# A decoder trunk on one core: casts of operand sums moved between the first products of the gates, pinned on ScalarE

## Chip, core and metric

The kernel runs on one core of a Trainium2 chip. The metric is the time of one execution in device microseconds. Before the change three runs took 1092.08, 1084.63 and 1091.85 us; their median is 1091.85 us.

## What is computed

One layer of a hybrid decoder, for 1024 prompt tokens and 8 x 4 sample tokens, all in float32:

```
h = rms(x);  z = h @ w_in                  # q, k, v and pooling columns
mix = concat(attention(q, k, v), pooling(u)) @ w_out
x = x + rms(mix)
f = rms(x);  f = (silu(f @ w_gate) * (f @ w_up)) @ w_down
x = x + rms(f)
x = x + sigmoid(x @ w_ple_gate) * (p @ w_ple)
```

The model width is 1024, p is 256 wide. The last line, the gates of the per-layer input, is where most of the change lies; its x is the sum x + rms(f) of the line before.

## The kernel before

**Tiles.** Features lie on the partitions, tokens along the free dimension, in three blocks of 352 tokens (g = 0, 1, 2). A tile called a half holds four of the eight feature groups of one block, 128 x 4 x 352; it lies in one of 28 slots. Every float32 operand of a matmul is split in a high part (a cast on ScalarE) and a low part (source minus high part on VectorE); a product is then three matmuls, high by high, high by low, low by high. `split` (L166) makes such a pair, at L167 (ScalarE) and L168 (VectorE).

**Seven products for four.** For blocks 0 and 1 together, the large matrix products are made in the 2 x 2 scheme with seven products instead of eight. Its operands on the token side are B11 and B21 (the two halves of block 0), B12 and B22 (those of block 1), and differences T1 to T4 of them. On the weight side it needs sums S1 to S4 of quarters of the weight, which GpSimd adds in place (L1123 for the gates, L339 for the down projection). Block 2 is multiplied directly.

**The down projection** is a list of steps, one per product and set of weight slabs, each made by `down7` (L1262). The last step of each product adds its four PSUM banks to kept tiles (`add`, L1276). Before the last steps of P2, S2 and S4, one addition of a whole half puts P1 and the kept partial sum of that product together.

**The normed residual** of each block comes from `ple_steps(g)` (L1339), a generator. It is handed to `chain`, and `turn` runs it piece by piece between matmuls by an estimate of VectorE's load; `finish` runs out what is left of it. For block 1 its end also makes the differences for the gates: `e_sum` (L1321) subtracts two halves on VectorE (L1330), `e_high` (L1332) casts the high part on ScalarE (L1335) and returns the function that makes the low part on VectorE (L1337).

**The gates.** First block 2: `ple_out` (L1440) for eight output groups, each followed by an embedding of block 0 (p @ w_ple, L1420 copies it out of PSUM). Then blocks 0 and 1. `ple_first` (L1454) makes, for the output groups a = 7, 5, 3, 1, a first product with B11, copies it to the kept tile p1 (L1463, ScalarE), yields, and then adds the product with B21 in the same PSUM bank; this second product therefore has to wait for the copy. `ple_end` (L1423) puts the sigmoid (L1433, ScalarE) and the two VectorE operations behind it (L1436: times the embedding; L1437: plus the residual), and SP sends the result out (L1438). The four first products are interleaved with each other and with embeddings of block 1 (`embeds`, L1512) at L1516 to L1529. Last comes `ple_rest` (L1468) for four pairs of output groups, with the other five products; these use T1 to T4, and the weight sums of `w_sums` (L1113), which are split at L167 and L168. The first pair's sums are made early; for the second, third and fourth, GpSimd's additions follow a split of half a raw weight (tile w), because they overwrite that raw weight.

**Order.** Each engine runs its instructions in a fixed order, which a scheduler of the framework chooses from the program's order and its own estimates. `tc.keep_in_program_order` pins an instruction at its place in the program. Matmuls are pinned by a flag. The names below end in numbers: b are PSUM banks, u halves of the down projection's sums (and later T1 to T4, in their places), fh and fl high and low parts, wh and wl those of weights, sh and sl those of weight sums, w halves of a weight's pair, p first products, pp embeddings, sg and yo the gates' results.

Of the kernel before, what the change touches and what calls it, by code (L numbers as in the profile page):

```python
# [61 lines left out]
def trunk_kernel(  # L62
# [316 lines left out]
    chains = []  # L379
# [867 lines left out]
    sums7 = {}  # L1247
# [14 lines left out]
    def down7(n):  # L1262
# [12 lines left out]
        def add(out, a, b):  # L1275
            ve.tensor_tensor(out, a, b, op=ALU.add)  # L1276

        onto = {"P2": "P2", "S2": "P1", "S4": "P1"}.get(k, k) if final else k
        if final and k in ("P2", "S2", "S4"):
            add(sums7[onto], sums7["P1"], sums7[k])  # L1280

        def part(j, e):
            wh, wl = need(WDN[k, e], 2)
            x = xops[OPERAND[k], e]
# [8 lines left out]
        for j in range(4):  # L1293
            if len(at) > 2:
                part(j, at[-1])
            else:
                banks[j] = bank()
                for e in at:
                    part(j, e)
            v = banks[j][:, :N]  # L1300
            u = {q: t[:, j, :] for q, t in sums7.items()}

            if n < len(FIVE + TWO):
                se.copy(u[k], v)  # L1304
            else:
                add(u[onto], u[onto], v)
            if final and k in ("P2", "S4"):
                finished(j, int(k == "S4"))
# [23 lines left out]
    def e_high(name):  # L1332
        src = {"T1": os_[0][0], "T2": os_[1][0], "T3": os_[0][1], "T4": os_[1][1]}[name]
        hi, lo = half(0, F32R, "fh"), half(0, F32R, "fl")
        se.copy(hi, src)  # L1335
        e7[name] = hi, lo
        return lambda: ve.tensor_tensor(lo, src, hi.bitcast(F32), op=ALU.subtract)  # L1337

    def ple_steps(g):  # L1339

        pl = half(g, F32R, "pl")
        pls[g] = pl[:, 0:2, :], pl[:, 2:4, :]
        for k in range(2):
            pr = tmp(NS[g], "pr")
            load(pr, p[:, k, OFF[g] : OFF[g + 1]])
            split(pl[:, k, :], pl[:, 2 + k, :], pr)
        x2s[g] = []
        for h in range(2):
            x2[g][h] = half(g, s="x2")
            load(x2[g][h], x1d[g][h])  # L1350
        r = yield from rstd_steps(acc3[g], 24 if g == 1 else 12)
        for h in range(2):
            yh, xh = os_[g][h], x2[g][h]
            ve.tensor_tensor(yh, yh, bc4(r), op=ALU.mult)
            ve.tensor_tensor(xh, xh, yh, op=ALU.add)
            yield 20, 0
            if g == 2:
                x2s[g].append(f_operand(xh, g))
            elif (g, h) != (1, 0):
                e7[f"B{h + 1}{g + 1}"] = f_operand(xh, g)  # L1360
            yield 10, 0
        if g == 1:
            lows = []
            for total, high, low in (("T1", (), 0), ("T2", (), 0), ("T4", ("T2",), 0), ("T3", ("T4",), 1), (None, ("T3", "T1"), 1)):
                lows += [e_high(name) for name in high]
                if total:
                    e_sum(total)
                yield 10, 0
                if low:
                    lows.pop(0)()  # L1370
                    yield 10, 0
            for f in lows:
                f()

    def downs(n, halves):
        hid[:] = old_hid
# [138 lines left out]

    next(firsts[0])  # L1516
    next(firsts[1])
    list(firsts[0])
    embeds(W1[7][0], range(4, KC))
    next(firsts[2])  # L1520
    list(firsts[1])
    next(firsts[3])
    list(firsts[2])
    until[0] = len(ITEMS)
    for a, _ in PAIRS[2:]:
        for j in RAW2[a]:
            w_load(j)
    embeds(W1[1][0], range(4))
    list(firsts[3])  # L1529
    finish(list(chains))  # L1530
    for a, b in PAIRS:
        ple_rest(a, b)

# [85 lines left out]
```

## Time and profile before

| | |
|---|---|
| profiled execution, device us | 1092.91 |
| its span, first to last instruction | 1090.8 |
| around the span | 2.1 |
| median of three runs | 1091.85 |
| lowest and highest run | 1084.63, 1092.08 |
| mean granted clock of TensorE | 0.995 |
| busy: PE, VectorE (DVE), ScalarE (ACT), GpSimd (POOL) | 1075.4, 825.4, 525.7, 285.2 us |

Times in the profile count from the first instruction of the span. Rows of the instructions in order of time have the start, the duration, the engine, the line, the operation, the output and inputs, and in brackets how long the engine had been idle before and what ended that. A wait has the engine and line that waited, what it waited for, the total, the number of times and the longest. A stretch has, for each engine, its busy time and number of instructions, then the granted clock of TensorE, the share of the DMA engines, and GB/s. Matmuls overlap: one that shows 0.32 us starts 0.16 us behind the one before it.

### The profile page before, as it was taken

The page shows a single profiled execution, that of the slowest core. Times are in us where ns is not written, and L with a number is a line of the kernel's source. Part 1 is how long each engine was busy: PE and PEld are TensorE (multiplying, and loading weights), DVE is VectorE, ACT ScalarE, POOL GpSimd, SP SyncE. Part 2 cuts the span into 40 slices and gives each one's busy share as a digit, 9 for nine tenths or more (in the row PEclk, how much of TensorE's full clock was granted, in tenths as well). Part 3 has the DMA queues.
Part 4 walks back from the last instruction along what each step waited for, and adds up shares of the span by engine and source line. Part 5 has one row for each costly group of instructions (what it writes and reads, how often), then busy time and mean ns, then how long its engine had stood idle before and what let it go on. Part 6 is the DMA issues. An engine that isn't in the chain of part 4 may idle for free.

```text
span 1090.8 us, 17447 instructions
## 1 busy us (share of the span) xinstructions
PE 1075.4 (99%) x6793; PEld 1058.9 (97%) x6793; DVE 825.4 (76%) x1229; ACT 525.7 (48%) x951; POOL 285.2 (26%) x213
## 2 busy tenths in 40 slices
PE   9999999999999999999999999999999999999898
PEld 8999988899999999999999999999999999999898
DVE  6766388887979767758758659668678777998978
ACT  8522367666755434334434434334335732575542
POOL 1054022200000122323224232332309096202060
PEclk9999999999999999999999999999999999999899
DMA  8221310542734212441533614515777955825422
GB/s 295 67 66 53 104 55 21 194 173 78 252 125 144 89 66 70 153 169 58 204 118 104 229 48 152 188 47 201 262 275 267 366 193 187 314 95 190 126 70 73
DMA packets 54162, 162.01 MB, mean 149 GB/s; under 512 B 5796, under 2 KB 20164, under 8 KB 54080
## 3 DMA queue, kind: packets, MB, share of 16 engines
q1 hardware_dynamic: 52752, 159.13, 41.4%
q10 hardware_dynamic: 1328, 1.77, 0.5%
q8 instruction: 53, 0.87, 0.3%
q14 instruction: 29, 0.24, 0.1%
HBM read 123.02 MB, written 37.86 MB: 147 GB/s over the span
## 4 chain that ended last, share of the span: by engine, by line
PE 94%; DVE 2%; ACT 1%; DMA 1%; issue 0%; SPq 0%; ACTq 0%; DVEq 0%
PE b L126 94%; PE b L120 1%; DVE ql L168 1%; DVE u L1276 1%; DMA xo<-xd 1%; DMA xr<-in_x_dram 0%; ACT a L771 0%; DVE u L1330 0%; DVE acc L921 0%; DVE yo L1437 0%; DVE st L168 0%; DVE a L811 0%; DVE mx L763 0%; ACT a L736 0%; ACT qh L167 0%
## 5 line engine op out<-in xcount | busy, mean ns | idle before, releaser
L126 PE MATMUL b<-fh,wh 128*128 128x352 f32 x716 | 232.1, 324 | 5.2 <-ACT p L1463 5.2
L126 PE MATMUL b<-fh,wl 128*128 128x352 f32 x716 | 232.5, 325 | 0.0
L126 PE MATMUL b<-fl,wh 128*128 128x352 f32 x716 | 230.7, 322 | 0.0
L1123 POOL TENSOR_TENSOR wr<-wr 128x512 f32<-128x512 f32 x47 | 68.4, 1456 | 546.3 <-DVE wl L168 516.0
L168 DVE TENSOR_TENSOR wl<-wr,wh 128x1024 fp32r<-128x1024 f32 (+1 forms) x123 | 162.8, 1326 | 53.2 <-ACT wh L167 52.9
L167 ACT CAST wh<-wr 128x1024 fp32r<-128x1024 f32 (+1 forms) x123 | 126.1, 1027 | 129.3 <-PE b L126 102.8
L126 PE MATMUL b<-xo,qh 128*128 128x352 f32 x616 | 148.2, 322 | 1.2 <-DMA xo<-xd 1.2
L126 PEld LDWEIGHTS b<-fh,wh 128*128 128x128 f32 x716 | 134.7, 188 | 5.4 <-ACT p L1463 5.4
L126 PEld LDWEIGHTS b<-fl,wh 128*128 128x128 f32 x716 | 136.4, 190 | 0.0
L126 PEld LDWEIGHTS b<-fh,wl 128*128 128x128 f32 x716 | 134.9, 188 | 0.0
L126 PE MATMUL b<-fh,sl 128*128 128x352 f32 x416 | 134.7, 324 | 0.0
L126 PE MATMUL b<-fh,sh 128*128 128x352 f32 x416 | 134.4, 323 | 0.0
L126 PE MATMUL b<-fl,sh 128*128 128x352 f32 x416 | 133.6, 321 | 0.0
L126 PE MATMUL b<-h,wh 128*128 128x352 f32 x480 | 111.9, 323 | 1.1 <-ACT h L495 0.8
L126 PEld LDWEIGHTS b<-xo,qh 128*128 128x128 f32 x616 | 107.3, 188 | 1.7 <-ACT u L1304 1.4
L126 PE MATMUL b<-xo,ql 128*128 128x352 f32 x308 | 99.7, 324 | 1.4 <-DVE ql L168 1.4
L339 POOL TENSOR_TENSOR wq<-wq,wq 128x512 f32<-128x512 f32 x44 | 76.5, 1774 | 69.0 <-DVE ql L168 58.9
L167 ACT CAST st<-c 128x352 fp32r<-128x352 f32 x55 | 26.8, 487 | 123.0 <-DVE c L1192 96.8
L168 DVE TENSOR_TENSOR sl<-wr,sh 128x1024 fp32r<-128x1024 f32 x47 | 58.2, 1238 | 35.3 <-ACT sh L167 33.5
L126 PE MATMUL b<-hid,wh 128*128 128x352 f32 x352 | 84.8, 322 | 0.0
L126 PEld LDWEIGHTS b<-h,wh 128*128 128x128 f32 x480 | 82.3, 188 | 2.5 <-DVE h L496 1.2
L126 PEld LDWEIGHTS b<-fl,sh 128*128 128x128 f32 x416 | 79.0, 190 | 0.0
(211 smaller groups left out, 2178.5 us busy)
## 6 DMA issues: line engine op xcount, KB each, us to landing
wr<-in_w_gu_dram SPq DMA_DIRECT2D x64, 512.0 KB, 3.4
xd<-st SPq DMA_DIRECT2D x35, 704.0 KB, 5.1
xo<-xd SPq DMA_DIRECT2D x35, 704.0 KB, 5.9
wr<-in_w_dn_dram SPq DMA_DIRECT2D x22, 512.0 KB, 4.1
wq<-in_w_dn_dram SPq DMA_DIRECT2D x20, 512.0 KB, 8.6
wr<-in_w_pg_dram SPq DMA_DIRECT2D x10, 512.0 KB, 3.8
x<-in_x_dram SPq DMA_DIRECT2D x6, 704.0 KB, 9.1
x1d<-x SPq DMA_DIRECT2D x6, 704.0 KB, 3.3
```

The source lines that it names most:

```text
L120: ins = te.transpose(out, src, ident)
L126: ins = te.matmul(*args, **kw)
L167: fix(se.copy(hi, src))
L168: fix(ve.tensor_tensor(lo, src, hi.bitcast(F32), op=ALU.subtract))
L339: ge.tensor_tensor(*(q_load(q, e)[:, i, :] for q in (out, a, b)), op=op)
L1123: ge.tensor_tensor(out, a, b, op=op)
L1276: ve.tensor_tensor(out, a, b, op=ALU.add)
```

## The change

```diff
@@ -1276,9 +1276,6 @@
             ve.tensor_tensor(out, a, b, op=ALU.add)
 
         onto = {"P2": "P2", "S2": "P1", "S4": "P1"}.get(k, k) if final else k
-        if final and k in ("P2", "S2", "S4"):
-            add(sums7[onto], sums7["P1"], sums7[k])
-
         def part(j, e):
             wh, wl = need(WDN[k, e], 2)
             x = xops[OPERAND[k], e]
@@ -1299,6 +1296,8 @@
                     part(j, e)
             v = banks[j][:, :N]
             u = {q: t[:, j, :] for q, t in sums7.items()}
+            if j == 0 and final and k in ("P2", "S2", "S4"):
+                add(sums7[onto], sums7["P1"], sums7[k])
 
             if n < len(FIVE + TWO):
                 se.copy(u[k], v)
@@ -1332,7 +1331,7 @@
     def e_high(name):
         src = {"T1": os_[0][0], "T2": os_[1][0], "T3": os_[0][1], "T4": os_[1][1]}[name]
         hi, lo = half(0, F32R, "fh"), half(0, F32R, "fl")
-        se.copy(hi, src)
+        tc.keep_in_program_order(se.copy(hi, src))
         e7[name] = hi, lo
         return lambda: ve.tensor_tensor(lo, src, hi.bitcast(F32), op=ALU.subtract)
 
@@ -1360,17 +1359,9 @@
                 e7[f"B{h + 1}{g + 1}"] = f_operand(xh, g)
             yield 10, 0
         if g == 1:
-            lows = []
-            for total, high, low in (("T1", (), 0), ("T2", (), 0), ("T4", ("T2",), 0), ("T3", ("T4",), 1), (None, ("T3", "T1"), 1)):
-                lows += [e_high(name) for name in high]
-                if total:
-                    e_sum(total)
+            for name in ("T1", "T2", "T4", "T3"):
+                e_sum(name)
                 yield 10, 0
-                if low:
-                    lows.pop(0)()
-                    yield 10, 0
-            for f in lows:
-                f()
 
     def downs(n, halves):
         hid[:] = old_hid
@@ -1515,19 +1506,27 @@
 
     next(firsts[0])
     next(firsts[1])
+    finish(list(chains))
+    low = e_high("T2")
     list(firsts[0])
     embeds(W1[7][0], range(4, KC))
     next(firsts[2])
+    low()
+    low = e_high("T4")
     list(firsts[1])
     next(firsts[3])
+    low()
+    low = e_high("T3")
     list(firsts[2])
     until[0] = len(ITEMS)
     for a, _ in PAIRS[2:]:
         for j in RAW2[a]:
             w_load(j)
+    low()
+    low = e_high("T1")
     embeds(W1[1][0], range(4))
     list(firsts[3])
-    finish(list(chains))
+    low()
     for a, b in PAIRS:
         ple_rest(a, b)
```

The differences T1, T2, T4, T3 are still made by the chain. Their high and low parts are no longer made there: each cast is written behind one of the first products and pinned at its place on ScalarE, and each low part is written one product further on. The chain is finished two first products on, ahead of the first cast, where it was finished behind the last of `ple_first`. In `down7` the whole-half addition is written behind the first PSUM bank of the step instead of ahead of the step. Nothing is added or taken away; the number of instructions on each engine is the same. PE's order is the same too. In the new kernel, lines behind the edits are smaller by up to 9 (L1463 is L1454, L1436 is L1427, L1337 is L1336).

On ScalarE, the place is the end of block 2's gates and the start of the first products. fh_10314 is the last high part of block 1's halves, b_10477 and b_10497 hold the first two first products (b_10464 and b_10483 in the new kernel). Before:

```order
L167 CAST fh_10314<-x_10091 128x1408
L1335 CAST fh_10381<-u_8421 128x1408
L1433 ACTIVATE sg_10405<-b_10359 128x352
L1420 COPY pp_10292<-b_10468 128x352
L1335 CAST fh_10401<-u_8652 128x1408
L1335 CAST fh_10449<-u_8482 128x1408
L1335 CAST fh_10452<-u_8567 128x1408
L1433 ACTIVATE sg_10462<-b_10419 128x352
L1463 COPY p_10476<-b_10477 128x352
L1463 COPY p_10476<-b_10497 128x352
```

and now:

```order
L167 CAST fh_10314<-x_10091 128x1408
L1424 ACTIVATE sg_10399<-b_10359 128x352
L1411 COPY pp_10292<-b_10455 128x352
L1454 COPY p_10463<-b_10464 128x352
L1424 ACTIVATE sg_10449<-b_10413 128x352
L1454 COPY p_10463<-b_10483 128x352
L1334 CAST fh_10497<-u_8421 128x1408
L167 CAST wh_10360<-a_10251 128x1024
```

All four casts stood ahead of the first copy; now the copy of the first product has none ahead of it, and T2's cast (u_8421) is the first, behind the second copy. T4's, T3's and T1's follow one by one further down.

On VectorE, the place is the low part of the first pair's weight sums (sl_10640, now sl_10639) to the half weight that the third pair's sums wait for (w_10697, of raw weight a_10495, now a_10481). Before:

```order
L168 TENSOR_TENSOR sl_10640<-wr_10129,sh_10639 128x1024
L1436 TENSOR_TENSOR sg_10622<-sg_10622,pp_10041 128x352
L1437 TENSOR_TENSOR yo_10623<-sg_10622,x_9805 128x352
L168 TENSOR_TENSOR sl_10644<-wr_10055,sh_10643 128x1024
L1436 TENSOR_TENSOR sg_10691<-sg_10691,pp_10041 128x352
L168 TENSOR_TENSOR w_10697<-a_10495,w_10697 128x512
```

and now:

```order
L168 TENSOR_TENSOR sl_10639<-wr_10129,sh_10638 128x1024
L1427 TENSOR_TENSOR sg_10617<-sg_10617,pp_10041 128x352
L1428 TENSOR_TENSOR yo_10618<-sg_10617,x_9805 128x352
L1336 TENSOR_TENSOR fl_10603<-u_8482,fh_10602 128x1408
L1336 TENSOR_TENSOR fl_10631<-u_8567,fh_10630 128x1408
L168 TENSOR_TENSOR sl_10643<-wr_10055,sh_10642 128x1024
L1427 TENSOR_TENSOR sg_10690<-sg_10690,pp_10041 128x352
L168 TENSOR_TENSOR w_10697<-a_10481,w_10697 128x512
```

The low parts of T3 (u_8482) and T1 (u_8567) have come in between; they stood some ten rows further up, close behind the differences.

On VectorE in the down projection, the one place where the whole-half addition moves is at the last step of S4 (u_8903 is its kept sum, ql_9865 the low part of its last weight set):

```order
 L921 TENSOR_TENSOR acc_9815<-acc_9815,sq_9818 128x352
+L168 TENSOR_TENSOR ql_9865<-wq_9231,qh_9864 128x512
+L921 TENSOR_TENSOR acc_9815<-acc_9815,sq_9822 128x352
 L1276 TENSOR_TENSOR u_8421<-u_8421,u_8903 128x1408
-L921 TENSOR_TENSOR acc_9815<-acc_9815,sq_9822 128x352
-L168 TENSOR_TENSOR ql_9866<-wq_9231,qh_9865 128x512
 L921 TENSOR_TENSOR acc_9815<-acc_9815,sq_9826 128x352
```

The addition goes behind that weight's low part and one small addition. Those of P2 and S2 stand where they stood.

On SP, the load of a_10481 (before a_10495) stands ahead of two outputs that it followed; the other loads of the last pairs follow at most one output later.

## Prediction

> **What bounds the kernel now.** I read the page first, then who waited for whom on PE alone, then the instructions in order of time around PE's longest wait, engine by engine.
>
> ```profile
> span 1090.8 us, 17447 instructions
> PE 1075.4 (99%) x6793; PEld 1058.9 (97%) x6793; DVE 825.4 (76%) x1229; ACT 525.7 (48%) x951; POOL 285.2 (26%) x213
> ...
> PE b L126 <- ACT p L1463: 5.2, 1, 5.2
> PE b L126 <- DVE ql L168: 1.4, 2, 1.2
> PE b L126 <- DMA xo<-xd: 1.2, 1, 1.2
> ```
>
> PE is busy for all but 15.4 us (1090.8 - 1075.4), so the change can only win what PE loses by waiting or by a slower clock. The one long wait inside the program is for the copy of a first product (L1463).
>
> ```profile
> 1020.12 0.32 PE L126 MATMUL b<-fh,wl 128*128 128x352 f32 x1
> 1025.60 0.66 PE L126 MATMUL b<-fh,wh 128*128 128x352 f32 x1 [5.15 <-ACT p L1463]
> ...
> 1028.99 0.49 PE L126 MATMUL b<-fh,wl 128*128 128x352 f32 x1
> 1029.28 0.65 PE L126 MATMUL b<-pl,wh 128*128 128x352 f32 x2
> ...
> 1041.06 4.03 PE L126 MATMUL b<-pl,a 128*128 128x352 f32 x24
> 1044.93 0.32 PE L126 MATMUL b<-fh,wh 128*128 128x352 f32 x1
> ...
> 1046.86 0.32 PE L126 MATMUL b<-fh,sh 128*128 128x352 f32 x1
> ```
>
> At full speed 24 matmuls take 1044.93 - 1041.06 = 3.87 us, 0.161 each. Without the wait the matmul of 1025.60 would have started at 1020.12 + 0.16 = 1020.28: 5.3 us are lost. From 1025.60 to 1046.86, where the rest of the gates begins with sums as weights (sh), lie 120 matmuls in 21.26 us, against 120 x 0.161 = 19.3: another 1.9 us went in the slow matmuls just behind the wait. The stretches show why (after each span: PE busy, PEld, DVE, ACT, POOL, then the granted clock):
>
> ```profile
> 936.00:938.00 2.00, 0.76 (x5) 0.76 (x6) 2.00 (x4) 2.00 (x3) 0.00 (x0) 1.00 1.00 353
> ...
> 1022.00:1024.00 2.00, 0.00 (x0) 0.00 (x0) 2.00 (x3) 1.83 (x3) 0.00 (x0) 0.70 0.00 0
> 1026.00:1028.00 2.00, 2.00 (x8) 2.00 (x8) 1.93 (x4) 0.00 (x0) 0.00 (x0) 0.50 0.43 98
> 1028.00:1030.00 2.00, 2.00 (x10) 2.00 (x9) 0.76 (x1) 0.77 (x1) 0.00 (x0) 0.60 0.73 259
> ```
>
> The granted clock is 0.50 from about 1022.8 (0.70 as a mean over 1022 to 1024) to about 1029.6, that is from 2.4 us after PE stopped, for 6.8 us. So this one stall costs 5.3 + 1.9 = 7.2 us. Why was the copy late? ScalarE's rows, then VectorE's:
>
> ```profile
> 1014.05 1.39 ACT L167 CAST fh<-x 128x1408 fp32r<-128x1408 f32 x1
> 1015.66 1.38 ACT L1335 CAST fh<-u 128x1408 fp32r<-128x1408 f32 x1 [0.22 <-DVE u L1330]
> ...
> 1020.67 1.36 ACT L1335 CAST fh<-u 128x1408 fp32r<-128x1408 f32 x1 [2.94 <-DVE u L1330]
> 1022.21 2.63 ACT L1335 CAST fh<-u 128x1408 fp32r<-128x1408 f32 x2 [0.17 <-DVE u L1330]
> 1024.75 0.46 ACT L1433 ACTIVATE sg<-b 128x352 f32<-128x352 f32 x1
> 1025.10 0.80 ACT L1463 COPY p<-b 128x352 f32<-128x352 f32 x2
> ```
>
> ```profile
> 1019.03 1.61 DVE L1330 TENSOR_TENSOR u<-x,u 128x1408 f32<-128x1408 f32 x1
> 1020.57 1.61 DVE L1330 TENSOR_TENSOR u<-x,x 128x1408 f32<-128x1408 f32 x1
> 1022.10 0.51 DVE L1436 TENSOR_TENSOR sg<-sg,b 128x352 f32<-128x352 f32 x1
> ```
>
> The first product ends at about 1018.5, but on ScalarE its copy stands behind three casts that wait for VectorE's differences T4 and T3 (L1330), the last of which ends at 1022.18. ScalarE idles 2.94 us there with the copy behind it.
>
> **The change, part by part.**
>
> *The casts (L1335) go behind the copies.* On ScalarE the row after the cast of 1014.05 is now a sigmoid, an embedding's copy, then the first product's copy. That is ready at about 1015.9, 1017.0 and 1018.5 + 0.45 = 1019.0, and PE wants it at 1020.28. The wait is gone: +5.3, and the 1.9 of clock with it. What is late next is VectorE: the embedding behind the second products waits for the PSUM bank that the L1436 row of 1022.10 reads, and VectorE's rows up to that one are the same, in the same order, without idle time. It ends at 1022.61; PE comes there at 1020.28 + 12 x 0.161 = 1022.2. I take 0.4 us; 0 if another bank is meant, 1.3 if it is the next L1436, which then ends at 1023.5. So the second products start at once, the embedding at 1022.66, and PE reaches the sums, 108 matmuls later, at 1040.06 instead of 1046.86: **6.8 us earlier**.
>
> *The casts themselves* (1.36 us each) fall between work that ScalarE has to wait with for PE anyway: replayed row by row, T2's ends at 1022.3, T4's at 1030.4, T3's at 1034.3, T1's at 1037.1, while their first matmuls come at 1042 and later. No copy of a first product is pushed past PE's need. Bounds 0 and 1.4 (one cast in front of one copy); I take 0.
>
> *The low parts* (L1337, two SBUF inputs of 128x1408 like the L1330 rows, 1.61 us, in steps of 1.54) move on VectorE too, and this is where I see the new price. T3's and T1's now stand between the low part of the first pair's sums (sl) and the weight half (w) that releases GpSimd's additions for the third pair of `ple_rest`. Before, these and the fourth pair's ran so, with the halves that release them at 1048.54 and 1057.45:
>
> ```profile
> 1048.54 0.68 DVE L168 TENSOR_TENSOR w<-a,w 128x512 fp32r<-128x512 f32 x1
> ...
> 1057.45 0.68 DVE L168 TENSOR_TENSOR w<-a,w 128x512 fp32r<-128x512 f32 x1
> ...
> 1058.57 1.31 DVE L1436 TENSOR_TENSOR sg<-sg,pp 128x352 f32<-128x352 f32 x1
> 1059.92 1.50 DVE L1437 TENSOR_TENSOR yo<-sg,x 128x352 f32<-128x352 f32 x1
> 1061.34 1.61 DVE L1436 TENSOR_TENSOR sg<-sg,pp 128x352 f32<-128x352 f32 x1
> 1062.98 1.50 DVE L1437 TENSOR_TENSOR yo<-sg,x 128x352 f32<-128x352 f32 x1
> 1064.40 1.21 DVE L168 TENSOR_TENSOR sl<-a,sh 128x1024 fp32r<-128x1024 f32 x1
> ```
>
> ```profile
> 1049.31 1.50 POOL L1123 TENSOR_TENSOR a<-a 128x512 f32<-128x512 f32 x1 [3.86 <-DVE w L168]
> 1050.88 3.53 POOL L1123 TENSOR_TENSOR a<-a,a 128x512 f32<-128x512 f32 x2
> 1054.49 2.15 POOL L1123 TENSOR_TENSOR a<-a 128x512 f32<-128x512 f32 x1
> 1058.21 1.29 POOL L1123 TENSOR_TENSOR a<-a 128x512 f32<-128x512 f32 x1 [1.57 <-DVE w L168]
> ...
> 1062.64 1.45 POOL L1123 TENSOR_TENSOR a<-a 128x512 f32<-128x512 f32 x1
> ```
>
> Each group of four additions starts 0.1 us behind the half's row on VectorE. While GpSimd adds, a VectorE addition of two SBUF tiles takes 1.3 to 1.6 us instead of 0.51 and ends 0.4 us behind the GpSimd row it met. The last VectorE row (sl of the third pair's sums, ends 1065.61) feeds the matmul that is 119 behind 1046.86, at 1066.0: a margin of 0.4 us only. Times from the start R of the sums' matmuls (1046.86 before, 1040.06 now):
>
> - the third pair's half ended at R + 2.4; now it stands behind the first pair's sl (ends 1036.8), two additions slowed by the second pair's group (38.3, 39.9), T3 (41.4), T1 (43.0), another sl (44.1), an addition (44.5), and ends at 1045.1 = R + 5.1;
> - the third pair's group then ends at about 1052.7 = R + 12.6 (before 1056.64, R + 9.8). ScalarE's cast of its sums waits for that, and three sigmoids queue behind this cast, so the first is done at about 1054.2;
> - the fourth pair's half meets the last row of that group and ends at 1053.3 (R + 13.2, before R + 11.3);
> - the four additions of the rows above start at 1054.2, each behind a row of the fourth pair's group, and end at about 1059.6; sl ends at 1060.8. PE wants it at R + 119 x 0.161 = 1059.2.
>
> So PE waits about **1.6 us** at the third pair's sums. Bounds: 0, if each of the four last rows of GpSimd comes 0.4 us sooner, and 4.4 (rivals). For the fourth pair's sums nothing behind this place is moved.
>
> A wait of 1.6 us lies between 1.2 us (PE's wait for ql, in the stretch from 936, where the clock stayed at 1.00) and 5.15 us; the drop came 2.4 us after the stop, so I take no clock loss. [...]
>
> *Transfers.* On SP's queue the first of the last four weight loads moves ahead of two outputs, the other three stay one output behind the addition that they followed. Their landing takes 3.8 us by the DMA view's median and the first use of the last is 10 us behind its issue: 0, at most the 0.4 us issue of one entry.
>
> ```profile
> a<-in_w_pg_dram SPq DMA_DIRECT2D x6, 512.0 KB, 3.8
> ```
>
> *The whole-tile addition (L1276).* Of the three, two keep their place on VectorE; the one of S4 moves behind a weight cast of 0.68 us. There PE does not wait:
>
> ```profile
> 960.00:980.00 20.00, 20.00 (x127) 20.00 (x126) 19.81 (x25) 16.76 (x29) 0.00 (x0) 1.00 0.26 81
> 961.75 1.62 DVE L1276 TENSOR_TENSOR u<-u,u 128x1408 f32<-128x1408 f32 x1
> ```
>
> It is 0: PE's full stretch covers it. Without that cover it would be a gain of 1.6 for the cast.
>
> **Sum.** 5.3 + 1.9 - 0.4 - 1.6 = 5.2 us less. The profiled run took 1092.91 us (2.1 around its span), so 1087.7 for such a run; it lies 1.1 above the median of the runs, 1091.85, which gives **1086.7**.
>
> **Rivals.** *No new wait:* the sums keep up, and the whole 6.8 comes: 1085.1. For it: the replay runs over some thirty rows, and 1.6 us of error in it suffice. Against: the margin is 0.4 us today and T3 and T1 put 3.1 us in front of it.
>
> *The sums become the bound and the clock drops again:* one mechanism, sl of the third pair late by more than 2.4 us. A wait s then also costs the half clock, by the one case seen (9.1 - s)/2; with s = 4.4 that is 4.4 + 2.4 = 6.8, all that was won, and from there on it is slower: s = 5.5 gives 5.5 + 1.8 - 6.8 = 0.5 more, 1092.4. It needs 2.8 us beyond my replay, four GpSimd rows at 2.15 instead of 1.45, as happens where VectorE casts 1024 columns among them. [...]
>
> *The change does not do what it says:* the copy is still late, because the sigmoid now ahead of it waits for its output buffer or VectorE's row of 1022.10 comes later than I have it: about 1091.9, no change. Against: the buffer's output was issued ten microseconds before.
>
> **How the numbers follow.** Chances: my forecast 0.5, no new wait 0.25, sums late with the clock 0.15, no change 0.1. The forecast's own range, 0.4 to 2.4 us of new wait, is 1085.4 to 1087.5. For 8 in 10 I go from 1081.0 to 1092.4: above, the two cases near 1092; below, because one of the three runs (1084.63) was 7 us under the others for a reason that the profile does not tell, and a median may land on such a run's side. A measurement tells about 1% (10.9 us) from no change, and no case reaches that: faster 0.05, for a second loss that goes with the first, within 1% 0.92, slower 0.03.
>
> **What would show it.** Right: no PE wait on L1454 (the copy's new line), no stretch at 0.50 around 1023 to 1030, ScalarE's copy before 1019.2, an embedding's wait of under 0.6 us, the matmuls on sums from about 1040, and a PE wait for sl (L168) of 1 to 2 us near 1059. Wrong: a PE wait of over 2.4 us with a clock under 1.00 behind it; the third pair's half (w) ending less than 3 us behind R; or PE still waiting for the copy.

## The result and the profile after

The changed kernel takes 1078.3 us in the median of 12 runs (1077.93 to 1086.59), the kernel before, in 12 runs of the same comparison, 1086.04 us (1083.54 to 1093.69). The ratio is 0.992, with a 95% interval from 0.9892 to 0.9948. That is 7.7 us faster, 0.7%, and below the predicted range, which began at 1081.0.

One thing has to be known to read any time here: the runs fall into two groups 8 us apart, because PE (TensorE) goes through the gate/up stage (the products with w_gate and w_up) at one of two paces. Over all comparisons the kernel before has 76 runs from 1082.7 to 1086.7 us (median 1084.3) and 25 from 1091.2 to 1095.4 us (median 1092.5); the changed kernel has 16 from 1077.6 to 1080.6 us (median 1078.3) and two, 1086.3 and 1086.6 us. The profile of before that the prediction read lies in the longer group; the profile after, 1077.93 us, in the shorter. Like against like, the change is worth 6.0 us (1084.3 to 1078.3).

The page of the profile after, its first lines:

```profile
span 1076.1 us, 17443 instructions
...
PE 1065.0 (99%) x6793; PEld 1049.4 (98%) x6793; DVE 829.1 (77%) x1229; ACT 526.2 (49%) x951; POOL 284.4 (26%) x213
```

PE's waits in it (engine and line, what it waited for, total, times, longest):

```profile
PE b L126 <- DVE ql L168: 1.6, 2, 1.2
...
PE b L126 <- DVE sl L168: 1.0, 1, 1.0
...
PE b L126 <- DMA xo<-xd: 0.7, 1, 0.7
```

The wait of 5.2 us for the copy is gone, and a wait of 1.0 us for sl is new. But PE is also busy for 10.4 us less (1075.4 to 1065.0), and the lost half clock explains only some 2 us of that. The rest is the pace. Stretches of 50 us of the gate/up stage (after each span: its length, PE's busy time and number of matmuls, the granted clock, the DMA share, GB/s), first of before, then of after:

```profile
220.00:270.00 50.00, 50.00 (x312) 1.00 0.34 122
740.00:790.00 50.00, 50.00 (x313) 1.00 0.66 235
```

```profile
220.00:270.00 50.00, 50.00 (x317) 1.00 0.36 127
740.00:790.00 50.00, 50.00 (x316) 1.00 0.69 250
```

PE is fully busy in all four, at a granted clock of 1.00, and still does 312 or 313 matmuls in one execution and 316 or 317 in the other: a step of 0.161 us against one of 0.159 (by the rows in order of time, 75 matmuls from 744.71 to 756.80 us before, 77 from 744.75 to 756.98 after). The stage is some 610 us long, so that is 8 us. PE, VectorE and ScalarE run the same instructions in the same order up to its end in both profiles, and only PE is slower: ScalarE's weight casts in it (L167, 128x1024) take 1049 ns before and 1050 after. Cut at the same places, the spans compare so. "Before again" is the unchanged kernel profiled once more, in an execution with the shorter step (first experiment). R is the start of the first matmul on weight sums of the gates.

| stretch | before | before again | after |
|---|---|---|---|
| start to PE's stop behind the gate/up stage | 834.28 | 826.82 | 826.26 |
| from there to the end of PE's last wait for ql | 102.96 | 101.81 | 101.98 |
| from there to R | 109.62 | 109.83 | 102.24 |
| R to the end | 43.94 | 43.74 | 45.62 |
| span | 1090.8 | 1082.2 | 1076.1 |

Of the 14.7 us between the two spans 8.0 are the pace of the first line, and 1.0 is the second line, which "before again" shows without the change. The change itself is in the last two lines: 7.4 us less ahead of R, 1.7 us more behind it, 5.7 us in all.

The start of the gates, after, in order of time on each engine:

```profile
1009.56 0.45 ACT L1454 COPY p<-b 128x352 f32<-128x352 f32 x1 [1.47 <-PE b L126]
...
1011.48 0.46 ACT L1454 COPY p<-b 128x352 f32<-128x352 f32 x1 [1.10 <-PE b L126]
1011.83 1.38 ACT L1334 CAST fh<-u 128x1408 fp32r<-128x1408 f32 x1
...
1011.12 0.32 PE L126 MATMUL b<-fh,wl 128*128 128x352 f32 x1
1011.28 0.32 PE L126 MATMUL b<-fh,wh 128*128 128x352 f32 x1
...
1013.04 0.32 PE L126 MATMUL b<-fh,wl 128*128 128x352 f32 x1
1013.20 0.48 PE L126 MATMUL b<-pl,wh 128*128 128x352 f32 x2
...
1013.09 0.51 DVE L1427 TENSOR_TENSOR sg<-sg,b 128x352 f32<-128x352 f32 x1
```

ScalarE copies the first product 1.3 us before PE wants it, and the cast of T2 comes behind both copies. The second product follows the first without a gap. So does the embedding at 1013.20, although VectorE's row (L1427) ends only at 1013.60: that row does not hold the embedding's bank.

The place of the new wait, after:

```profile
1030.48 0.32 PE L126 MATMUL b<-fh,sh 128*128 128x352 f32 x1
...
1030.36 3.15 DVE L1336 TENSOR_TENSOR fl<-u,fh 128x1408 fp32r<-128x1408 f32 x2
...
1035.00 0.68 DVE L168 TENSOR_TENSOR w<-a,w 128x512 fp32r<-128x512 f32 x1
...
1042.55 1.11 DVE L168 TENSOR_TENSOR w<-a,w 128x512 fp32r<-128x512 f32 x1
...
1044.63 0.79 DVE L1427 TENSOR_TENSOR sg<-sg,pp 128x352 f32<-128x352 f32 x1 [0.54 <-ACT sg L1424]
1045.45 1.50 DVE L1428 TENSOR_TENSOR yo<-sg,x 128x352 f32<-128x352 f32 x1
1046.87 1.61 DVE L1427 TENSOR_TENSOR sg<-sg,pp 128x352 f32<-128x352 f32 x1
1048.52 1.49 DVE L1428 TENSOR_TENSOR yo<-sg,x 128x352 f32<-128x352 f32 x1
1049.93 1.21 DVE L168 TENSOR_TENSOR sl<-a,sh 128x1024 fp32r<-128x1024 f32 x1
...
1041.82 1.29 POOL L1123 TENSOR_TENSOR a<-a 128x512 f32<-128x512 f32 x1
...
1051.20 0.43 PE L126 MATMUL b<-fh,sl 128*128 128x352 f32 x1 [1.04 <-DVE sl L168]
```

Two low parts (T3, T1) start at R and take 3.15 us of VectorE. The third pair's half ends at R + 5.2, GpSimd's group behind it at R + 12.6, the fourth pair's half at R + 13.2, the four VectorE rows beside GpSimd's last group at R + 19.5, and sl at R + 20.7, where PE waits for it.

### The profile page after: what moved, and what is told of

The parts are those of the page before. It is cut to its first block, busy times and chain, and to the rows that moved or that the text cites. A ratio compares the mean times of both kernels' runs of the same rounds, so it can differ in the third digit from the quotient of the medians.

```text
span 1076.1 us, 17443 instructions
## 1 busy us (share of the span) xinstructions
PE 1065.0 (99%) x6793; PEld 1049.4 (98%) x6793; DVE 829.1 (77%) x1229; ACT 526.2 (49%) x951; POOL 284.4 (26%) x213
## 4 chain that ended last, share of the span: by engine, by line
PE 90%; DVE 6%; issue 2%; ACT 1%; DMA 1%; SPq 0%; ACTq 0%; DVEq 0%
PE b L126 89%; DVE sl L168 1%; DVE ql L168 1%; DVE sg L1427 1%; PE b L120 1%; DVE yo L1428 1%; DVE u L1276 1%; DMA xo<-xd 0%; DVE p L1464 0%; ACT a L771 0%; DMA xr<-in_x_dram 0%; DVE st L168 0%; DVE acc L921 0%; DVE c L1095 0%; DVE w L168 0%
## 5 line engine op out<-in xcount | busy, mean ns | idle before, releaser
L126 PE MATMUL b<-fh,wl 128*128 128x352 f32 x716 | 229.5, 320 | 0.0
L1123 POOL TENSOR_TENSOR wr<-wr 128x512 f32<-128x512 f32 x47 | 67.6, 1439 | 534.0 <-DVE wl L168 510.1
L167 ACT CAST wh<-wr 128x1024 fp32r<-128x1024 f32 (+1 forms) x123 | 126.3, 1028 | 122.7 <-PE b L126 95.8
L167 ACT CAST st<-c 128x352 fp32r<-128x352 f32 x55 | 26.8, 488 | 122.9 <-DVE c L1192 96.6
L126 PEld LDWEIGHTS b<-fh,sl 128*128 128x128 f32 x416 | 78.0, 188 | 1.3 <-DVE sl L168 1.3
```

Of the source, the lines that this page charges most:

```text
L126: ins = te.matmul(*args, **kw)
L167: fix(se.copy(hi, src))
L1123: ge.tensor_tensor(out, a, b, op=op)
```

## The experiments

The theory to test had three parts. A: the places of the casts carry the whole gain, through the stall and the half clock behind it; T3's and T1's low parts, standing ahead of the third pair's half, make the new wait; and the other 8 us are a pace of PE that no edit chose. The rivals were that the addition took part, that the pace came with the change, and, as the runs went on, that VectorE's whole row and not its order makes the wait.

Since the pace differs from one execution to the next, a kernel's effect is read in its profile from the end of PE's last wait for ql: to R, from R to the last product, and from there to the end (us). The last column is the median of the runs of the shorter group, with their number, then the number in the longer one. The step can change where PE stops (see the stop in mid-stage), so it moves the stretch to R (638 matmuls) by up to 1.4 us and the next one (239) by up to 0.5 us with no edit at all: "after again" has 317 matmuls from 960 to 1010 us where "after" has 314, and is 0.7 us shorter to R. R to end is steadier, 45.55 to 45.66 us in the six profiles whose program from R on is that of the change.

| kernel | to R | R to last product | to the end | R to end | runs |
|---|---|---|---|---|---|
| before | 109.62 | 38.51 | 5.43 | 43.94 | 1084.3 (76), 25 |
| before again | 109.83 | 37.97 | 5.77 | 43.74 | 1084.3 (7), 3 |
| addition alone | 110.42 | 38.24 | 5.44 | 43.68 | 1084.4 (8), 2 |
| casts alone | 101.91 | 39.42 | 6.13 | 45.55 | 1078.0 (5), 5 |
| after | 102.24 | 39.69 | 5.93 | 45.62 | 1078.3 (16), 2 |
| after again | 101.55 | 39.65 | 6.00 | 45.65 | among those |
| low parts later | 102.30 | 42.88 | 5.46 | 48.34 | 1081.7 (5), 5 |
| sums first | 102.24 | 38.24 | 6.87 | 45.11 | 1078.4 (6), 4 |
| no low parts | 102.29 | 38.50 | 5.43 | 43.93 | 1076.0 (4), 1 |
| nine copies | 107.12 | 39.70 | 5.91 | 45.61 | 1083.6 (1), 0 |
| twelve copies | 109.85 | 39.38 | 6.20 | 45.58 | 0, one of 1095.2 |
| stop in mid-stage | 102.24 | 39.72 | 5.94 | 45.66 | see there |
| low parts earlier | 102.71 | 38.85 | 6.02 | 44.87 | 1078.3 (5), 0 |
| both edits | 102.98 | 38.50 | 5.94 | 44.44 | 1077.0 (10), 2 |

**Before again.** No edit.

> The kernel before, unchanged, profiled once more. Theory A (PE steps at one of two paces in a whole execution, and the shown profile of before had the slower): the run times fall into the same two groups as the twelve shown with the result, about 1083.5 to 1086.1 us and 1091.9 to 1093.7 us; if this profile is a quick one, its gate/up stage (first to last product of the loop) is about 8 us shorter than the 620.6 us of the shown profile, near 612, while from the gates on the PE wait of about 5.15 us for the first copy and the stretch at half clock are there as before. Theory B (the 8 us came with the change): a quick profile of before does not occur in the gate/up stage; it stays near 620 us.

Measured: seven runs from 1083.2 to 1085.0 us and three from 1092.1 to 1095.4. The profile, 1084.32 us, does 316 and 317 matmuls in the two stretches shown above, and is 7.5 us shorter up to the stop behind the gate/up stage; PE's wait for the copy is 5.15 us as before, and the gates differ by 0.2 us. So the kernel before has the shorter pace too: the 8 us did not come with the change.

**The casts alone, and the addition alone.** The move of the whole-half addition taken back (shown here), or made alone:

```diff
         onto = {"P2": "P2", "S2": "P1", "S4": "P1"}.get(k, k) if final else k
+        if final and k in ("P2", "S2", "S4"):
+            add(sums7[onto], sums7["P1"], sums7[k])
+
...
-            if j == 0 and final and k in ("P2", "S2", "S4"):
-                add(sums7[onto], sums7["P1"], sums7[k])
```

> The change without its second part: the whole-tile addition stands where it stood before, the casts stand as after. Theory A (the casts' places carry all of the gain): 6 to 7 us below before, within 1 us of after. Rival (the addition behind the first product took part in it): at least 2 us slower than after.

> The second part of the change alone: the whole-tile addition behind the first product, the casts where they were before. Theory A: no difference to before (within 0.2%). Rival (the addition frees PE or VectorE in the down products): 2 us or more faster than before.

Measured: with the casts alone 101.91 us to R and 45.55 behind it, with the addition alone 110.42 and 43.68. The groups say the same: 1078.0 and 1084.4 us. The raw medians, 1083.05 and 1084.62 us, do not show it, because five of ten runs of the one and two of ten of the other fell in the longer group; read alone, the first would have hidden most of the effect of the casts. With the addition alone the stretch to R is even 0.6 us longer than in before again: the half clock behind the same wait of 5.15 us lasted until 6.1 us after PE's restart, not 5.0. So no gain from the addition shows, and the casts carry all of it.

**Low parts later.** T3's and T1's low parts written behind the split of the third pair's half, and pinned there:

```diff
     made = {}
+    lows = []
...
                 split(*made[i], raws[js[0]][:, 4:8, :])
+                while lows:
+                    tc.keep_in_program_order(lows.pop(0)())
...
-    low()
-    low = e_high("T1")
+    lows += low, e_high("T1")
     embeds(W1[1][0], range(4))
     list(firsts[3])
-    low()
```

> The change, with the low parts of T3 and T1 written behind the split of the third pair's half, so that VectorE splits the half before it subtracts. Theory A (the two subtractions ahead of that split made GpSimd's sums of the third pair late, and with them the low part of the sums that PE waited 1.04 us for): GpSimd's third group starts about 3 us earlier after the first product on the sums, the wait for that low part goes, 1.0 us faster than after. Rival (the wait is set by VectorE's whole row there, whatever its order): the wait stays within 0.3 us, or turns up at the first product that uses the low part of T3 or T1, and the time is that of after or more.

Measured: GpSimd's third group does start 2.8 us sooner (R + 2.5 instead of R + 5.3), and yet PE's wait grows to 2.38 us. Rows of VectorE and GpSimd (R is 1038.96 here):

```profile
1040.64 0.69 DVE L168 TENSOR_TENSOR w<-a,w 128x512 fp32r<-128x512 f32 x1
...
1041.68 5.34 DVE L1339 TENSOR_TENSOR fl<-u,fh 128x1408 fp32r<-128x1408 f32 x2
...
1053.44 0.68 DVE L168 TENSOR_TENSOR w<-a,w 128x512 fp32r<-128x512 f32 x1
...
1060.37 1.21 DVE L168 TENSOR_TENSOR sl<-a,sh 128x1024 fp32r<-128x1024 f32 x1
...
1042.98 5.18 POOL L1126 TENSOR_TENSOR a<-a,a 128x512 f32<-128x512 f32 x2
1048.25 2.15 POOL L1126 TENSOR_TENSOR a<-a 128x512 f32<-128x512 f32 x1
```

The two low parts now run beside GpSimd's additions and take 5.34 us instead of 3.15; the additions beside them take 5.18 instead of 4.40. GpSimd ends 1.2 us sooner, not 2.8, and VectorE reaches the fourth pair's half 2.4 us later (R + 14.5, was R + 12.1), on which sl depends. That the wait goes when the low parts stand behind the half is refuted: there they cost more. The wait of 2.38 us also brought the clock down:

```profile
1059.10:1061.60 2.50, 0.15 (x1) 0.93 0.11 42
1061.60:1064.70 3.10, 3.07 (x10) 0.50 0.09 29
1064.70:1070.00 5.30, 5.30 (x34) 1.00 0.19 68
```

**Sums first.** An order edge puts the late sl ahead of the four VectorE rows of 1044.63 to 1048.52, which only make outputs:

```diff
-            ve.tensor_tensor(sg[:, v], sg[:, v], pp[:, v], op=ALU.mult)
+            gated = ve.tensor_tensor(sg[:, v], sg[:, v], pp[:, v], op=ALU.mult)
+            if m == KC - 2 and g == 0:
+                behind(gated, third[1][0])
...
```

Here gated is the first product of a gate with its embedding in the first pair, third[1][0] the low part of the third pair's sums, and behind adds an edge that orders the two on VectorE without a semaphore.

> The change, with one added order edge: VectorE makes the low part of the sums that PE waited 1.04 us for ahead of the products with the embeddings of the step before (four instructions, 1044.63 to 1050.0 us in the profile after), not behind them. Theory A1 (VectorE's whole row from the first product on the sums is what is late, so an urgent piece must pass the four that nobody waits for): the low part is ready by about 1046.5 us on the clock of the profile after, PE's wait of 1.0 us goes, no new one comes; from PE's last wait of VectorE's ql to the end 146.8 us where after has 147.9. Rival (the row only turns over, and what is pushed back is waited for next): a wait of 0.5 us or more on another piece, the end unmoved.

Measured: no wait for sl, and 38.24 us from R to the last product, 1.45 less. But the end follows that product 0.94 us later than after, and R to end is 45.11: half of the expected gain, too little to show in the runs (1078.4 us against 1078.3). The last product and VectorE's last row:

```profile
1077.73 0.32 PE L126 MATMUL b<-fh,sl 128*128 128x352 f32 x1
...
1081.46 0.34 DVE L1444 TENSOR_TENSOR yo<-sg,x 128x176 f32<-128x176 f32 x1
```

VectorE's last row starts 3.73 us behind the last product; in the profile of before it was 2.28 (1087.65 - 1085.37), after 2.76 (1072.93 - 1070.17). What was pushed back is not waited for by PE, but it is still there when PE is done.

**No low parts.** T3's and T1's high parts take the place of their low parts:

```diff
-        hi, lo = half(0, F32R, "fh"), half(0, F32R, "fl")
+        hi = half(0, F32R, "fh")
+        lo = half(0, F32R, "fl") if name in ("T2", "T4") else hi
...
+        if lo is hi:
+            return lambda: None
```

> The change, with the low parts of T3 and T1 left out: their high parts are multiplied twice, so TensorE does as many products and VectorE two subtractions (3.15 us) less, and the values of this part differ. Theory of the prediction (these two subtractions ahead of the third pair's split make PE wait): GpSimd's third group starts 3 us earlier after the first product on the sums, PE's wait of 1.04 us is gone. Rival (the row beside GpSimd is as long anyway): a wait of at least 0.7 us stays.

Measured: no wait for sl in the list of PE's waits, and R to end 43.93 us, as in the kernel before (43.68 to 43.94). So these two subtractions are the whole price behind R: 1.7 us, of which PE loses 1.2 at sl (the wait of 1.04 and the 0.16 by which matmuls overlap) and 0.5 come in the tail. VectorE's row says how, from R to the end of VectorE's last instruction (its length, VectorE's busy time and number of instructions), before, after, and without the low parts:

```profile
1046.86:1087.99 41.13, 37.46 (x62) 1.00 0.16 57
...
1030.48:1073.28 42.80, 41.04 (x64) 1.00 0.19 68
...
1031.07:1072.20 41.13, 37.46 (x62) 1.00 0.20 71
```

VectorE works 3.6 us more after the change, the two subtractions and rows that run slower beside GpSimd (two sl, 1.89 and 2.31 us after, 1.37 and 1.72 before). Of these, 1.9 us fill time in which it was idle before, and its row ends 1.7 us later; the program ends 2.8 us behind that row in all three. In the kernel before they lay ahead of R, in and right behind the stall: its four low parts start from 1022.5 to 1031.5 us, and R is 1046.86. Together with the two runs above this says what the price is: mainly work moved into a row that has little idle time left up to the end. The order in the row is worth less: sums first, with 41.05 us of work in it, ended 0.5 us sooner.

**A stop of chosen length.** Copies of 128 x 352 that nothing needs, ahead of the copy of the first product on ScalarE, nine or twelve:

```diff
-        se.copy(p1s[0][:, a // 2, :], ps[:, :N])
+        if a == KC - 1:
+            for _ in range(9):
+                tc.keep_in_program_order(se.copy(p1s[0][:, 0, :], x2[0][0][:, 0, :]))
+            tc.keep_in_program_order(se.copy(p1s[0][:, a // 2, :], ps[:, :N]))
+        else:
+            se.copy(p1s[0][:, a // 2, :], ps[:, :N])
```

> The change, with nine copies of 128 x 352 that nothing needs, put on ScalarE ahead of the copy of the first product, so that PE waits again for that copy, here about 3.0 us. Theory A (the half clock follows any stop of PE of over 2.4 us, the time from the stop to the first half-clock sample before, and lasts until 4 us after PE goes on): the profile shows a stretch at a clock of 0.5 about there, and the stage is longer than after by the wait and 2.0 us more, 5.0 us. Rival C (only a stop of over 4.4 us or so costs clock): no stretch at 0.5, longer than after by the wait alone, 3.0 us.

> As the one before with twelve copies: a wait of about 4.1 us. Theory A: a stretch at a clock of 0.5, 6.1 us longer than after from PE's last wait of ql to the end. Rival C: none, 4.1 us longer. If this one has the stretch and that with nine copies has not, the limit lies between 3.0 and 4.1 us.

Measured: PE waits 3.14 and 4.71 us, and the stretch to R is 4.9 and 7.6 us longer than after: 1.7 and 2.9 us more than the waits. The clock in half-microsecond stretches, with nine copies (PE stopped at 1012.19, went on at 1015.33):

```profile
1015.50:1016.00 0.50, 0.50 (x4) 1.00 0.77 287
1016.00:1016.50 0.50, 0.50 (x4) 0.55 0.42 106
...
1019.00:1019.50 0.50, 0.50 (x3) 0.53 0.00 0
1019.50:1020.00 0.50, 0.50 (x5) 1.00 0.00 0
```

and with twelve (stopped at 1021.16, went on at 1025.87):

```profile
1024.00:1024.50 0.50, 0.00 (x0) 1.00 0.00 0
1024.50:1025.00 0.50, 0.00 (x0) 0.63 0.50 186
...
1031.00:1031.50 0.50, 0.50 (x3) 0.54 0.00 0
1031.50:1032.00 0.50, 0.50 (x5) 1.00 0.00 0
```

Between its edges each drop shows 0.50 (the stretches from 1016.50 to 1019.00 with nine copies, from 1025.00 to 1031.00 with twelve), so a mean clock of 0.55 is taken as 0.9 of the stretch at one half (2 x (1 - 0.55)): the first drop runs from 1016.05 to 1019.47, 3.4 us, and begins only after PE had gone on; the second from 1024.63 to 1031.46, 6.8 us. Half of the part of the drop in which PE works is an estimate of what it costs: 1.7 us, and (1031.46 - 1025.87)/2 = 2.8, against the 1.7 and 2.9 measured. Rival C, no clock loss below about 4.4 us, is refuted. Theory A had the first total (5.0 expected, 4.9 measured) but not its form, and missed the second by 1.5 us, since the wait was 0.6 longer than expected and the drop lasted longer behind it.

**After again, a stop in mid-stage, low parts earlier.** These three shared one chip and its runs of the kernel before. The first has no edit.

> The changed kernel once more, on the chip and in the rounds of the two that follow. Theory A (the step of PE in the gate/up stage falls one way or the other in each execution, whatever the kernel; the twelve times of the result had few of the slow kind by chance): two groups, near 1078.2 and near 1086.5 us, 8 to 9 us apart, the slow one in about a third of the runs as in the kernel before. Rival (the change itself makes the quick step likelier): one slow run in ten or fewer, while before shows a third.

Measured: five runs from 1077.6 to 1078.9 us and one of 1086.28, which is the profiled one; that profile's gate/up stage has 312 and 313 matmuls in the two stretches. So the changed kernel has both paces. On this chip the kernel before had none of 15 runs in the longer group, on another 10 of 31: the share varies by chip or call, and over all it is 25 of 101 for the kernel before and 19 of 70 for the kernels of the last column that move the casts. The rival, that the change makes the short step likelier, is not borne out by these shares; the 18 runs of the changed kernel alone, two in the longer group, are too few to exclude it. Here, where the kernel before showed one group only, the ratio is 0.9946, from 0.9933 to 0.996.

The second:

```diff
         p5 = product(s["S1"], f7["T1"])
+        if hold[0]:
+            held, t = bank(), tmp(n, "held")
+            tc.keep_in_program_order(se.copy(t, p5[:, :n]))
+            tc.keep_in_program_order(te.transpose(held[:, :P], t[:, :P], ident))
```

hold[0] is set for one pass in the middle of the stage.

> The change, with one wait of PE put into the middle of the gate/up stage, near 520 us: ScalarE copies the product that PE has just ended, and PE transposes a piece of that copy, which nothing reads, before it goes on; about 1 us. Theory A' (any stop of PE redraws its step, which then holds until the next stop): the profile can show different steps before and after that place, and the times fall into up to four groups, both halves quick near 1079, one of them slow near 1083, both slow near 1087.5 us. Rival (the step belongs to the execution or the stage, not to PE's last stop): two groups 8 to 9 us apart, as without it, 1 us later, and one step on both sides of the wait.

Measured: PE stops once, and the step is another behind it.

```profile
511.81 0.32 PE L126 MATMUL b<-fh,sl 128*128 128x352 f32 x1
513.98 0.33 PE L1199 MATMUL b<-c,held 128*128 128x128 f32 x1 [1.85 <-ACT held L1198]
```

```profile
460.00:510.00 50.00, 50.00 (x317) 1.00 0.35 127
520.00:570.00 50.00, 50.00 (x315) 1.00 0.41 149
...
740.00:790.00 50.00, 50.00 (x315) 1.00 0.64 232
```

317 matmuls in 50 us ahead of the stop, 315 behind it up to the end of the stage, a third step of 0.160 us that no other profile shows in this stage; in each of the thirteen others the count holds throughout. The eleven runs lie from 1081.4 to 1087.0 us with no gap over 1.6 us, where the changed kernel without the stop leaves nothing between 1080.6 and 1086.3. The stage behind it says the same. The kernel before stops for 1.2 us at 834.28, and its 312 or 313 matmuls become 314 or 315; sums first has no stop there and keeps its 312. From 870 to 920 us, before, then sums first:

```profile
870.00:920.00 50.00, 50.00 (x314) 1.00 0.54 179
```

```profile
870.00:920.00 50.00, 50.00 (x312) 1.00 0.54 176
```

So in these profiles the step can change where PE stops, and where it does not stop, it holds. The four groups that were expected did not show as such, which fits three steps instead of two. What sets the step at a restart stays open.

The third writes the casts of T4, T3 and T1 one place earlier, with their low parts:

```diff
     list(firsts[0])
+    low()
+    low = e_high("T4")
     embeds(W1[7][0], range(4, KC))
     next(firsts[2])
     low()
-    low = e_high("T4")
+    low = e_high("T3")
     list(firsts[1])
     next(firsts[3])
     low()
-    low = e_high("T3")
+    low = e_high("T1")
     list(firsts[2])
...
-    low()
-    low = e_high("T1")
     embeds(W1[1][0], range(4))
-    list(firsts[3])
     low()
+    list(firsts[3])
```

> The change with the casts of T4, T3 and T1 each written one place earlier among the first products, and their low parts with them. Theory A2 (the change pays about 1.7 us from the first product on the sums to the end, because two low parts of 1.58 us that VectorE had made in the stall now lie behind that point; VectorE has 1.1 us of idle time ahead of it, before 1020.92 us in the profile after): from that product to the end 44.0 to 44.6 us, as before had 43.7 to 43.9 and after 45.6; no wait for sl, or one below 0.5 us; 1.0 to 1.7 us faster than after in the quick group. Rival (the casts come between the embeddings' copies on ScalarE, so PE waits for a bank or for a copy of a first product): a wait of 0.5 us or more before the first product on the sums, and no gain.

Measured: R to end 44.87 us, 0.75 less than after and short of the expected 44.0 to 44.6; PE's wait for sl is 0.2 us. But the stretch to R is 0.5 us longer, and the runs, 1078.3 us, are those of the changed kernel. A third of a microsecond is not to be told apart here.

**Both edits**, low parts earlier and sums first.

> The change with both edits: the casts of T4, T3 and T1 one place earlier, and the low part of the third pair's sums ahead of the four products that nobody waits for. By the theory that VectorE's row from the first product on the sums sets the end: no wait for sl, from that product to the end 44.3 to 44.9 us, no better than the earlier casts alone, since a piece that passes others only turns the row over and 0.8 us is what the earlier casts took out of it. Rival (PE's wait and the tail behind its last product are separate losses, so the two gains add): 43.9 us, as before had.

Measured: R to end 44.44 us, no wait for sl, so the gains behind R do not add up to the 43.9 of the rival. They do add up, though, against the theory's "no better than the earlier casts alone": 0.51 of sums first and 0.75 of the earlier casts are 1.26, and 1.18 came. Ahead of R there is a small new wait:

```profile
PE b L126 <- DVE wl L177: 0.4, 1, 0.4
```

The ten runs of the shorter group have a median of 1077.0 us, 1.4 under the changed kernel's 1078.3, and the ratio to before is 0.9934 (0.9908 to 0.996). Of the kernels that compute the same values it has the shortest time, but its interval overlaps with that of the change on another chip (0.9933 to 0.996), so that it is better than the change is likely and not shown.

## Why the prediction was wrong, and where it was right

**The step that failed is the base.** The text took 5.2 us from the profiled execution and came to 1086.7 by way of the median, "it lies 1.1 above the median of the runs, 1091.85". Both that execution and that median were of the longer pace; of the three runs shown, 1084.63 was of the shorter, and the prediction put its 7 us down to "a reason that the profile does not tell". The profile could have given a hint: at a clock of 1.00 it has 312 or 313 matmuls in 50 us of the gate/up stage and 314 or 315 in the stages behind it. Why an execution gets the one pace or the other stays open; that it does, without any edit, "before again" shows. Of the 8.4 us between 1086.7 and 1078.3, 7.6 are the base (1091.85 against 1084.3) and 0.8 the terms (6.0 against 5.2, by the shorter groups). The low end repeats the slip: the same 5.2 us below the run of 1084.63 is 1079.4, which also lay outside the range.

**The stall, +5.3, and the clock, +1.9: right.** The stretch to R fell by 7.4 us, 109.62 to 102.24, against 7.2. The 1.9 belong to the profile that was read: in the two other profiles of the same stall (before again, the addition alone) the half clock lasted until 5.0 and 6.1 us after PE's restart, not 4.0, and cost, by an estimate of half that time, 2.5 and 3.1 us. The copy came when the replay had it: 1.27 us ahead of PE's need, where the prediction had 1.28 (1020.28 - 1019.0).

**The embedding, -0.4: absent.** The row that was held responsible ended 0.4 us behind the embedding's start, and PE did not wait. The text had named this case ("0 if another bank is meant"), and it was that one.

**The new wait, -1.6: right in size, in part by luck, and half right in kind.** The replay of three engines met the trace to a tenth of a microsecond at every step (R + 5.2, 12.6, 13.2, 19.5, 20.7, against 5.1, 12.6, 13.2, 19.5, 20.7). PE's side was miscounted: the matmul that waits for sl is the 122nd behind R, not the 119th, so PE wants it at R + 19.5 instead of R + 19.2 and loses 1.2 us, not 1.6. (By the same count the margin before was 0.9 us, not 0.4.) Another 0.5 us came in the tail behind the last product, which the text did not look at. Together R to end grew by 1.7 to 1.9 us; that what was overlooked makes up for what was counted too long is luck. As for the cause, the text blamed the place of the two low parts ahead of the third pair's half. Low parts later, sums first and no low parts showed that it is mainly their 3.15 us in a row of VectorE that has little idle time from R to the end; order in that row gave back 0.5 of the 1.7 us.

**The casts, the transfers, the addition, 0: right.** No cast stands ahead of a copy that PE waits for, no transfer has a wait that before had not (xo is 0.7 us, was 1.2), and the addition alone shows no gain.

**The rivals.** No new wait did not happen. The one with the clock, a wait for sl of more than 2.4 us that takes half clock with it, was a real danger: low parts later made a wait of 2.38 us, and the clock fell for 3.4 us behind it. Its price was put at (9.1 - s)/2 from one case; the six stops that cost clock show that a drop lasts 3.4 or 6.8 us and begins 2.0 to 4.4 us behind the stop, so that the formula does not carry over to other stops.

## What to carry to other kernels

Before taking a gain from a base, find out whether the runs of the base are one group: two profiles of the same kernel, cut at the same places, tell pace from work, and an effect is read from the stage that the edit touches. When a stall goes, the work that ran in it goes somewhere; add up what the engine has to do from there to the end, and how much idle time it has left for it. What does not fit comes back, in waits or in the tail: here 1.7 of 3.6 us, of which another order gave back 0.5. And of a wait that stays, ask not only how long it is but whether it is long enough for the clock: here 1.85 us was not, 2.38 us was.

## What the runs showed of the hardware

**PE has more than one step at full clock.** In the gate/up stage a matmul of 352 columns follows the one before it after 0.159 us (after, before again: 316 or 317 matmuls in 50 us) or 0.161 us (before: 312 or 313), and after the stop in mid-stage after 0.160 (315), each time at a granted clock of 1.00. In these profiles the step holds from one stop of PE to the next, here over 600 us, and is worth 8 us (834.28 us up to the stop behind the stage before, 826.26 after). What picks it stays open.

**The clock falls for 3.4 or 6.8 us.** By short stretches, the drops to 0.50 behind PE's waits last 3.4 us (waits of 2.38 us, low parts later, and 3.14, nine copies) and 6.8 us (one wait of 4.71 us, twelve copies, and three of 5.15: before, before again, the addition alone). They begin 2.0 us (low parts later), 2.4 (before), 3.3 (before again), 3.5 (twelve copies), 3.9 (nine copies) and 4.4 us (the addition alone) behind the stop, with the wait of 3.14 us only after PE had gone on. Waits of 1.04 us (for sl, after), 1.25 (for ql, before) and 1.85 (the stop in mid-stage) had none: the clock stayed at 1.00 from 1049 to 1060, from 935 to 945 and from 511 to 523 us. What sets the two lengths and the start of a drop was not shown.

**VectorE and GpSimd take longer beside each other, by kind of work.** A low part of 128 x 1408 takes 1.6 us alone (1.61 in the median of four, before) and 2.7 beside GpSimd's additions (5.34 for two, low parts later), and GpSimd's addition of 128 x 512 for the sums (L1123), 1.28 at the least before, takes 2.6 beside it (5.18 for two, low parts later). A 128 x 352 operation of VectorE on two SBUF tiles takes 0.5 alone (0.52 at 1048.11 us before) and 1.3 to 1.6 beside them (1058.57 to 1062.98 us before); one with an input in PSUM takes 0.51 beside them too (L1464 at 1036.04 us after, while GpSimd adds from 1035.76 to 1037.27).
